# RMSNorm with repeated rows: three-tile runs of stores and loads, wide operations by tile, gamma on the load queue

## The chip, the cores and the metric

The kernel runs on one core of a Trainium2 chip. The metric is the device time of one execution in microseconds, as the median of several runs. A profile of a single execution gives the span from its first to its last recorded event and what every engine and DMA queue did in it.

## The reference

Each row of x (2048 float32) is divided by its root mean square and multiplied by gamma, and each result row stands in the output twice.

```python
x_rep = np.repeat(x, 2, axis=1)                     # x: 8 x 512 x 2048
rms = np.sqrt((x_rep ** 2).mean(axis=-1, keepdims=True) + 1e-6)
return (x_rep / rms * gamma[None, None, :]).astype(np.float32)
```

The input is 33.6 MB and the output, with every row twice, 67.1 MB.

## The kernel before

The 4096 rows are cut into 8 tiles of 512 rows: 128 partitions with K = 4 rows each. A tile has one SBUF buffer `y` of 8 row slots per partition (64 KB). The four x rows are loaded into slots 4 to 7 (L45 to L53); the results go to slots 0, 2, 4 and 6, and their copies to slots 1, 3, 5 and 7, so that x rows are overwritten once they have been used. The whole of the 8 slots is then stored in one piece (L55 to L59). There are three such buffers (L39), so a load of tile j waits for the store of tile j - 3.

The work of one row, by `compute` (L82):

- `square` (L61): ScalarE squares the row into a PSUM scratch tile and sums it at the same time (L64), and takes the root of the mean plus eps (L68).
- `scale` (L71): VectorE takes the reciprocal (L73) and multiplies the row by it and by gamma in one operation (L74).
- `repeat` (L79): ScalarE copies the result into the slot beside it, for the last row of a group VectorE does (L80). ScalarE squares row k + 1 before it copies row k.

The order on each engine is the order of the program (`manual_schedule`, L94); an instruction waits only for what it reads or overwrites. All loads and stores are issued by SyncE (SP) in the order of the program, on one DMA queue, q1: load 0 in two halves, loads 1 and 2, then stores 0 and 1, loads 3 and 4, stores 2 and 3, loads 5 and 6, stores 4 and 5, load 7 in two halves, store 6 and store 7 in two halves (L107 to L116). A store waits on SP for its tile's copies, and what is behind it on SP waits with it. Gamma is one row: ScalarE issues it in four pieces on its own queue, q10 (L97 to L100), and GpSimd broadcasts it to all partitions (L101).

```python
    for i in range(ntiles):
        parts = 2 if i == ntiles - 1 else 1
        for k in range(0, K, K // parts):
            compute(i, k, k + K // parts)
            store(i, k, k + K // parts)

        if i % 2 == 1:
            for j in (i + 2, i + 3):
                if j < ntiles:
                    load(j, nc.sync, parts=2 if j + 1 == ntiles else 1)
```

Of the kernel before, what the change touches and what calls it, by code (L numbers as in the profile page):

```python
# [1 line left out]

# [4 lines left out]


@with_exitstack
def kernel(  # L10
    ctx: ExitStack,
    tc: tile.TileContext,
    x: bass.AP,
    gamma: bass.AP,
    out: bass.AP,
):
    nc = tc.nc
    P = nc.NUM_PARTITIONS
    f32 = mybir.dt.float32
    Act = mybir.ActivationFunctionType  # L20
    Alu = mybir.AluOpType

    B, S, D = x.shape
    Bo, So, Do = out.shape
    R = So // S
    assert R == 2 and D == Do and B == Bo and So == S * R
    eps = 1e-6
    inv_d = 1.0 / float(D)


    K = 4
    N = B * S
    assert N % (P * K) == 0
    ntiles = N // (P * K)
    x_t = x.rearrange("b s d -> (b s) d").rearrange("(n p k) d -> n p k d", p=P, k=K)
    out_t = out.rearrange("b s d -> (b s) d").rearrange("(n p j) d -> n p (j d)", p=P, j=K * R)

    singles = ctx.enter_context(tc.tile_pool(name="singles", bufs=1))
    rows = ctx.enter_context(tc.tile_pool(name="rows", bufs=3))  # L39
    junk = ctx.enter_context(tc.tile_pool(name="junk", bufs=1, space=bass.MemoryType.PSUM))  # L40
    small = ctx.enter_context(tc.tile_pool(name="small", bufs=8))

    ys = []

    def load(i, eng, parts=1):  # L45


        y = rows.tile([P, K * R, D], f32, name="y")
        step = K // parts
        for k in range(0, K, step):  # L50
            at = K * (R - 1) + k
            eng.dma_start(out=y[:, at : at + step, :], in_=x_t[i, :, k : k + step, :])  # L52
        ys.append(y)  # L53

    def store(i, k0, k1):  # L55
        nc.sync.dma_start(  # L56
            out=out_t[i, :, R * k0 * D : R * k1 * D],
            in_=ys[i][:, R * k0 : R * k1, :].rearrange("p j d -> p (j d)"),
        )  # L59

    def square(i, k):  # L61
        sq = junk.tile([P, D], f32, name="sq")
        ss = small.tile([P, 1], f32, name="ss")
        nc.scalar.activation(  # L64
            out=sq[:], in_=ys[i][:, K * (R - 1) + k, :], func=Act.Square, accum_out=ss[:]
        )
        rms = small.tile([P, 1], f32, name="rms")
        nc.scalar.activation(out=rms[:], in_=ss[:], func=Act.Sqrt, scale=inv_d, bias=eps_t[:])  # L68
        return rms

    def scale(i, k, rms):  # L71
        rstd = small.tile([P, 1], f32, name="rstd")
        nc.vector.reciprocal(out=rstd[:], in_=rms[:])  # L73
        nc.vector.scalar_tensor_tensor(  # L74
            out=ys[i][:, R * k, :], in0=ys[i][:, K * (R - 1) + k, :], scalar=rstd[:], in1=gamma_b[:],
            op0=Alu.mult, op1=Alu.mult,
        )

    def repeat(i, k, copy):  # L79
        copy(out=ys[i][:, R * k + 1, :], in_=ys[i][:, R * k, :])  # L80

    def compute(i, k0, k1):  # L82

        rms = square(i, k0)
        for k in range(k0, k1):
            scale(i, k, rms)
            if k + 1 < k1:
                rms = square(i, k + 1)
                repeat(i, k, nc.scalar.copy)
            else:  # L90
                repeat(i, k, nc.vector.tensor_copy)


    ctx.enter_context(tc.manual_schedule())  # L94
    load(0, nc.sync, parts=2)
    gamma_b = singles.tile([P, D], f32, name="gamma_b")
    for c in range(0, D, D // 4):  # L97
        nc.scalar.dma_start(
            out=gamma_b[0:1, c : c + D // 4], in_=gamma[c : c + D // 4].partition_broadcast(1)
        )  # L100
    nc.gpsimd.partition_broadcast(out_ap=gamma_b[:], in_ap=gamma_b[0:1, :])  # L101
    eps_t = singles.tile([P, 1], f32, name="eps_t")
    nc.vector.memset(eps_t, eps)  # L103
    load(1, nc.sync)
    load(2, nc.sync)

    for i in range(ntiles):  # L107
        parts = 2 if i == ntiles - 1 else 1
        for k in range(0, K, K // parts):
            compute(i, k, k + K // parts)  # L110
            store(i, k, k + K // parts)

        if i % 2 == 1:
            for j in (i + 2, i + 3):
                if j < ntiles:
                    load(j, nc.sync, parts=2 if j + 1 == ntiles else 1)  # L116


# [1 line left out]
_INS = ['x', 'gamma']  # L120
_OUTS = [((8, 1024, 2048), 'float32')]


# [23 lines left out]
```

## Time and profile before

| What | Value |
|---|---|
| median of 7 runs | 239.88 us (239.81 to 240.41) |
| the profiled execution | 239.55 us, of which its span is 237.8 us |
| HBM read, written | 33.56 MB, 67.11 MB; 423 GB/s over the span |
| ScalarE (ACT) | 32 squares of 1871 ns, 32 roots of 295, 23 copies of 1888, two table loads of 1283 |
| VectorE (DVE) | 32 scales of 2352 ns, 32 reciprocals of 162, 9 copies of 1226 |
| GpSimd (POOL) | one broadcast of 2292 ns |
| SP waits for copies | 7 times, 121.4 us in all |
| SP waits for an earlier store, before a load | 5 times, 72.8 us in all |

In the profile, each digit of a line of slices is the busy share of 1/40 of the span in tenths. A group of instructions is given as line, engine, operation, output and inputs with their shapes, count, then the busy time in us, the mean of one in ns, and the idle time of the engine before them with what ended most of it. "SPq" is the queue in which SP issues DMAs. A wait of SP is not a loss as such: the DMA engines work on what was issued earlier.

### The profile page before, as it was taken

To read this page: it belongs to the slowest core of one execution; us is meant where nothing else is said; L and a number is where in the kernel's file an instruction comes from. 1 tells how busy PE (TensorE), PEld (TensorE's weight loads), DVE (VectorE), ACT (ScalarE), POOL (GpSimd) and SP (SyncE) were. 2 spreads that over 40 slices of the span, in tenths; PEclk is the share of its full clock that TensorE was granted. 3 is DMA by queue.
4 is the path that set the end of the run, shared out by engine and by line. 5 is a ranking of instruction groups with operands and counts; after the bars stand their busy time and mean duration, and the time that the engine had idled before them with its cause. 6 is when DMAs were issued, how large, how long until landed. Compare 5 with 4: busy or idle time off the path is not lost.

```text
span 237.8 us, 301 instructions
## 1 busy us (share of the span) xinstructions
DVE 90.8 (38%) x74; ACT 115.3 (49%) x121; POOL 2.5 (1%) x5
## 2 busy tenths in 40 slices
DVE  0086977864000084967000007696600009910000
ACT  2699999990000299997000049999500049700000
POOL 0300000000000000000000000000000000000000
DMA  7999998989899999989898999989898999999996
GB/s 265 436 447 441 441 441 353 529 353 507 375 397 436 419 430 437 529 353 529 353 496 353 441 419 442 496 364 518 353 518 364 394 430 499 441 397 419 430 430 265
DMA packets 2746, 100.69 MB, mean 423 GB/s; under 512 B 308, under 2 KB 308, under 8 KB 312
## 3 DMA queue, kind: packets, MB, share of 16 engines
q1 hardware_dynamic: 2736, 100.66, 98.6%
q14 instruction: 2, 0.02, 0.0%
q10 hardware_dynamic: 8, 0.01, 0.0%
HBM read 33.56 MB, written 67.11 MB: 423 GB/s over the span
## 4 chain that ended last, share of the span: by engine, by line
DMA 66%; ACT 15%; DVE 6%; issue 1%; SPq 0%; DVEq 0%
DMA out_dram<-y 40%; DMA y<-in_x_dram 25%; ACT sq L64 7%; ACT y L80 5%; DVE y L74 5%; ACT rms L68 1%; ACT L68 1%; DVE y L80 1%; DVE rstd L73 0%; SPq L52 0%; DVEq L74 0%; SPq L56 0%
## 5 line engine op out<-in xcount | busy, mean ns | idle before, releaser
L64 ACT ACTIVATE sq<-y 128x2048 f32<-128x2048 f32 x32 | 59.9, 1871 | 84.8 <-DMA y<-in_x_dram 84.8
L74 DVE SCALAR_TENSOR_TENSOR y<-y,rstd,gamma_b 128x2048 f32<-128x2048 f32 x32 | 75.3, 2352 | 1.2 <-DVE rstd L73 0.2
L73 DVE RECIPROCAL rstd<-rms 128x1 f32<-128x1 f32 x32 | 5.2, 162 | 115.6 <-ACT rms L68 115.6
L80 ACT COPY y<-y 128x2048 f32<-128x2048 f32 x23 | 43.4, 1888 | 3.7 <-DVE y L74 3.7
L80 DVE COPY y<-y 128x2048 f32<-128x2048 f32 x9 | 11.0, 1226 | 0.3
L68 ACT ACTIVATE rms<-ss,eps_t 128x1 f32<-128x1 f32 x32 | 9.4, 295 | 1.0
L64 ACT ACTIVATION_READ_ACCUMULATOR sq<-y 128x1 f32 x32 | 6.0, 186 | 0.0
L101 POOL PARTITION_BROADCAST gamma_b<-gamma_b x1 | 2.3, 2292 | 8.3 <-DMA gamma_b<-in_gamma_dram 8.3
L64 ACT ACT_TABLE_LOAD x1 | 1.3, 1283 | 2.1 <-issue 2.1
L68 ACT ACT_TABLE_LOAD x1 | 1.3, 1283 | 0.0
L103 DVE MEMSET eps_t<- 128x1 f32 x1 | 0.1, 59 | 0.8 <-PEq L131 0.8
L131 POOL MEMSET const-float32-0.0<- 128x1 f32 x1 | 0.1, 99 | 0.2 <-issue 0.2
L131 POOL MEMSET const-bfloat16-1.0<- 128x1 bf16 x1 | 0.1, 101 | 0.0
L131 POOL MEMSET const-uint8-127<- 128x1 uint8 x1 | 0.1, 101 | 0.0
L131 POOL MEMSET const-float32-1.0<- 128x1 f32 x1 | 0.1, 98 | 0.0
## 6 DMA issues: line engine op xcount, KB each, us to landing
y<-in_x_dram SPq DMA_DIRECT2D x6, 4096.0 KB, 25.0
y<-in_x_dram SPq DMA_DIRECT2D x4, 2048.0 KB, 9.6
out_dram<-y SPq DMA_DIRECT2D x2, 4096.0 KB, 26.6
out_dram<-y SPq DMA_DIRECT2D x7, 31.5
gamma_b<-in_gamma_dram ACTq DMA_DIRECT2D x4, 2.0 KB
```

The lines of the kernel that those rows point to most:

```text
L64: nc.scalar.activation(out=sq[:], in_=ys[i][:, K * (R - 1) + k, :], func=Act.Square, accum_out=ss[:])
L68: nc.scalar.activation(out=rms[:], in_=ss[:], func=Act.Sqrt, scale=inv_d, bias=eps_t[:])
L73: nc.vector.reciprocal(out=rstd[:], in_=rms[:])
L74: nc.vector.scalar_tensor_tensor(out=ys[i][:, R * k, :], in0=ys[i][:, K * (R - 1) + k, :], scalar=rstd[:], in1=gamma_b[:], op0=Alu.mult, o ...
L80: copy(out=ys[i][:, R * k + 1, :], in_=ys[i][:, R * k, :])
L101: nc.gpsimd.partition_broadcast(out_ap=gamma_b[:], in_ap=gamma_b[0:1, :])
L103: nc.vector.memset(eps_t, eps)
L131: nc = _bacc.Bacc("TRN2", target_bir_lowering=False, num_devices=1)
```

## The change

- **Order on SP.** Loads 0 to 2, stores 0 to 2, loads 3 to 5, stores 3 and 4, loads 6 and 7, stores 5 to 7. Only load 0 is still in two halves; store 7, like the others, is one piece.
- **Gamma.** Seven pieces (one of 512 elements, six of 256) on SP's queue: six between the halves of load 0, the last one behind the second half. They land in a small tile of two partitions, and GpSimd broadcasts two halves of 1024 columns.
- **Tables.** ScalarE's table with the square root is loaded ahead of all else, so that the second load of a table falls away. GpSimd sets `eps_t` and a tile of -0.5.
- **Tiles 0 and 3, by rows.** ScalarE sums two rows (Square with accumulation), takes both roots in one operation, and the other two likewise; VectorE takes reciprocals of two columns and scales.
- **Tiles 1, 2, 4, 6 and 7, mixed.** ScalarE squares several rows in one wide operation into slots that are still free (3 rows in tiles 1, 2 and 6; 2 in tile 4; 4 in tile 7) and sums the others as before; VectorE sums the squares in one wide reduce; GpSimd turns the four sums into (mean + eps) ** -0.5 by two small operations on 128x4; VectorE scales the four rows. The sums of the next tile are put into ScalarE's order after the root where `ahead` says so.
- **Tile 5.** All four rows are squared in one operation, reduced by VectorE, and turned by GpSimd; ScalarE scales each row by a Copy with a scale per partition, VectorE multiplies all four by gamma in one operation, and GpSimd makes the copy of all four rows.
- **Copies.** All copies of a tile come after its scales. Tiles 0 and 4: VectorE copies four rows at once. Tiles 1, 2, 3 and 7: ScalarE two, VectorE two. Tile 6: ScalarE two and two.

The diff, cut to its core:

```diff
@@ -42,78 +42,167 @@
     ys = []
-    def load(i, eng, parts=1):
-        y = rows.tile([P, K * R, D], f32, name="y")
-        step = K // parts
-        for k in range(0, K, step):
-            at = K * (R - 1) + k
-            eng.dma_start(out=y[:, at : at + step, :], in_=x_t[i, :, k : k + step, :])
-        ys.append(y)
-    def store(i, k0, k1):
+    def new_tile():
+        ys.append(rows.tile([P, K * R, D], f32, name="y"))
+    def load(i, k0, k1):
         nc.sync.dma_start(
-            out=out_t[i, :, R * k0 * D : R * k1 * D],
-            in_=ys[i][:, R * k0 : R * k1, :].rearrange("p j d -> p (j d)"),
-        )
-    def square(i, k):
+            out=ys[i][:, K * (R - 1) + k0 : K * (R - 1) + k1, :], in_=x_t[i, :, k0:k1, :]
+        )
+    def store(i):
+        nc.sync.dma_start(out=out_t[i], in_=ys[i].rearrange("p j d -> p (j d)"))
+    H = K // 2
+    x_at = K * (R - 1)
+    def total(i, k, ss):
         sq = junk.tile([P, D], f32, name="sq")
-        ss = small.tile([P, 1], f32, name="ss")
         nc.scalar.activation(
-            out=sq[:], in_=ys[i][:, K * (R - 1) + k, :], func=Act.Square, accum_out=ss[:]
-        )
-        rms = small.tile([P, 1], f32, name="rms")
-        nc.scalar.activation(out=rms[:], in_=ss[:], func=Act.Sqrt, scale=inv_d, bias=eps_t[:])
-        return rms
-    def scale(i, k, rms):
-        rstd = small.tile([P, 1], f32, name="rstd")
-        nc.vector.reciprocal(out=rstd[:], in_=rms[:])
-        nc.vector.scalar_tensor_tensor(
-            out=ys[i][:, R * k, :], in0=ys[i][:, K * (R - 1) + k, :], scalar=rstd[:], in1=gamma_b[:],
-            op0=Alu.mult, op1=Alu.mult,
-        )
-    def repeat(i, k, copy):
-        copy(out=ys[i][:, R * k + 1, :], in_=ys[i][:, R * k, :])
-    def compute(i, k0, k1):
-        rms = square(i, k0)
+            out=sq[:], in_=ys[i][:, x_at + k, :], func=Act.Square, accum_out=ss[:, k : k + 1]
+        )
+    def square(i, k0, k1):
+        nc.scalar.activation(
+            out=ys[i][:, k0:k1, :], in_=ys[i][:, x_at + k0 : x_at + k1, :], func=Act.Square
+        )
+    def reduce(i, k0, k1, ss):
+        nc.vector.tensor_reduce(
+            out=ss[:, k0:k1], in_=ys[i][:, k0:k1, :], op=Alu.add, axis=mybir.AxisListType.X
+        )
+    def root(k0, k1, ss):
+        at = ss[:, k0:k1]
+        nc.gpsimd.tensor_scalar(
+            out=at, in0=at, scalar1=inv_d, scalar2=eps, op0=Alu.mult, op1=Alu.add
+        )
+        nc.gpsimd.tensor_tensor(out=at, in0=at, in1=power_t[:, k0:k1], op=Alu.pow)
+    def scale(i, k0, k1, rstd):
         for k in range(k0, k1):
-            scale(i, k, rms)
-            if k + 1 < k1:
-                rms = square(i, k + 1)
-                repeat(i, k, nc.scalar.copy)
-            else:
-                repeat(i, k, nc.vector.tensor_copy)
+            nc.vector.scalar_tensor_tensor(
+                out=ys[i][:, R * k, :], in0=ys[i][:, x_at + k, :], scalar=rstd[:, k : k + 1],
+                in1=gamma_b[:], op0=Alu.mult, op1=Alu.mult,
+            )
+    def repeat(i, k0, k1, copy=nc.scalar.copy):
+        y_r = ys[i].rearrange("p (k r) d -> p k r d", r=R)
+        copy(out=y_r[:, k0:k1, 1, :], in_=y_r[:, k0:k1, 0, :])
+    def columns():
+        return small.tile([P, K], f32, name="ss")
     ctx.enter_context(tc.manual_schedule())
-    load(0, nc.sync, parts=2)
+    assert ntiles == 8
     gamma_b = singles.tile([P, D], f32, name="gamma_b")
-    for c in range(0, D, D // 4):
-        nc.scalar.dma_start(
-            out=gamma_b[0:1, c : c + D // 4], in_=gamma[c : c + D // 4].partition_broadcast(1)
-        )
-    nc.gpsimd.partition_broadcast(out_ap=gamma_b[:], in_ap=gamma_b[0:1, :])
+    cuts = [0, *range(D // 4, D + 1, D // 8)]
+    for _ in range(3):
+        new_tile()
+    gamma_row = singles.tile([64, D // 2], f32, name="gamma_row")
+    def gamma_half(c):
+        at = 32 * (c // (D // 2))
+        return gamma_row[at : at + 1, :]
+    def gamma_piece(c0, c1):
+        at = c0 % (D // 2)
+        nc.sync.dma_start(
+            out=gamma_half(c0)[:, at : at + c1 - c0], in_=gamma[c0:c1].partition_broadcast(1)
+        )
+    power_t = singles.tile([P, K], f32, name="power_t")
+    nc.gpsimd.memset(power_t, -0.5)
     eps_t = singles.tile([P, 1], f32, name="eps_t")
-    nc.vector.memset(eps_t, eps)
-    load(1, nc.sync)
-    load(2, nc.sync)
-    for i in range(ntiles):
-        parts = 2 if i == ntiles - 1 else 1
-        for k in range(0, K, K // parts):
-            compute(i, k, k + K // parts)
-            store(i, k, k + K // parts)
-        if i % 2 == 1:
-            for j in (i + 2, i + 3):
-                if j < ntiles:
-                    load(j, nc.sync, parts=2 if j + 1 == ntiles else 1)
+    nc.gpsimd.memset(eps_t, eps)
+    nc.scalar.preload_act_table(Act.Sqrt)
+    load(0, 0, H)
+    for c0, c1 in zip(cuts[:-2], cuts[1:-1]):
+        gamma_piece(c0, c1)
+    load(0, H, K)
+    gamma_piece(cuts[-2], cuts[-1])
+    for c0 in (0, D // 2):
+        nc.gpsimd.partition_broadcast(out_ap=gamma_b[:, c0 : c0 + D // 2], in_ap=gamma_half(c0))
+    load(1, 0, K)
+    load(2, 0, K)
+    def root_quick(k0, k1, ss):
+        at = ss[:, k0:k1]
+        nc.scalar.activation(out=at, in_=at, func=Act.Sqrt, scale=inv_d, bias=eps_t[:])
+        nc.vector.reciprocal(out=at, in_=at)
+    def by_rows(i, copies):
+        ss = [columns() for _ in range(R)]
+        for h, k0 in enumerate(range(0, K, H)):
+            for k in range(k0, k0 + H):
+                total(i, k, ss[h])
+            root_quick(k0, k0 + H, ss[h])
+            scale(i, k0, k0 + H, ss[h])
+        for k0, k1, copy in copies:
+            repeat(i, k0, k1, copy)
+        store(i)
+    def sums(i, by_row):
+        ss = columns()
+        square(i, by_row, K)
+        for k in range(by_row):
+            total(i, k, ss)
+        return i, by_row, ss
+    def mixed(given, copies, ahead=None):
+        i, by_row, ss = given
+        reduce(i, by_row, K, ss)
+        root(0, K, ss)
+        if ahead is not None:
+            ahead = sums(*ahead)
+        scale(i, 0, K, ss)
+        for k0, k1, copy in copies:
+            repeat(i, k0, k1, copy)
+        store(i)
+        return ahead
+    whole = ((0, K, nc.vector.tensor_copy),)
+    shared = ((0, H, nc.scalar.copy), (H, K, nc.vector.tensor_copy))
+    by_scalar = ((0, H, nc.scalar.copy), (H, K, nc.scalar.copy))
+    by_rows(0, whole)
+    two = mixed(sums(1, 1), shared, ahead=(2, 1))
+    mixed(two, shared)
+    for j in (3, 4, 5):
+        new_tile()
+        load(j, 0, K)
+    by_rows(3, shared)
+    _, _, ss = mixed(sums(4, H), whole, ahead=(5, 0))
+    for j in (6, 7):
+        new_tile()
+        load(j, 0, K)
+    reduce(5, 0, K, ss)
+    root(0, K, ss)
+    for k in range(K):
+        nc.scalar.activation(
+            out=ys[5][:, R * k, :], in_=ys[5][:, x_at + k, :], func=Act.Copy, scale=ss[:, k : k + 1]
+        )
+    y_r = ys[5].rearrange("p (k r) d -> p k r d", r=R)
+    nc.vector.tensor_tensor(
+        out=y_r[:, :, 0, :], in0=y_r[:, :, 0, :],
+        in1=gamma_b[:].rearrange("p (k d) -> p k d", k=1).to_broadcast([P, K, D]), op=Alu.mult,
+    )
+    repeat(5, 0, K, nc.gpsimd.tensor_copy)
+    store(5)
+    last = mixed(sums(6, 1), by_scalar, ahead=(7, 0))
+    mixed(last, shared)
 # ---- launch: one core; inputs and outputs as the reference has them ----
```

## The prediction

> **What bounds the kernel now.** I read the page first: engine shares, the slices and the queue.
>
> ```profile
> span 237.8 us, 301 instructions
> ...
> DVE 90.8 (38%) x74; ACT 115.3 (49%) x121; POOL 2.5 (1%) x5
> ...
> DMA  7999998989899999989898999989898999999996
> ...
> q1 hardware_dynamic: 2736, 100.66, 98.6%
> ```
>
> No compute engine is busy half the span; the one DMA queue, q1, holds the 16 DMA engines for 98.6% of it. Next, the stages, in the view by windows (length, busy time of DVE, ACT and POOL with counts, PE clock, DMA share, GB/s):
>
> ```profile
> 1.70:3.00 1.30, 0.00 (x0) 0.91 (x1) 0.00 (x0) 1.00 0.96 227
> ...
> 72.00:88.00 16.00, 3.90 (x4) 5.87 (x7) 0.00 (x0) 1.00 1.00 430
> 92.00:128.00 36.00, 16.26 (x13) 18.78 (x20) 0.00 (x0) 1.00 1.01 437
> 130.00:146.00 16.00, 3.61 (x4) 5.58 (x7) 0.00 (x0) 1.00 1.00 430
> 150.00:186.00 36.00, 16.56 (x13) 19.07 (x20) 0.00 (x0) 1.00 1.01 437
> ...
> 235.00:237.80 2.80, 0.00 (x0) 0.00 (x0) 0.00 (x0) 1.00 0.11 47
> ```
>
> Loads alone (72 to 88, 130 to 146) run at 430 GB/s and stores alone at 437, with compute beside them or not. So neither the direction nor the engines set the rate. Only the start (227 GB/s) and the end are below it. Last, the queue's own issues in order of time:
>
> ```profile
> 26.54 15.13 SPq L56 DMA_DIRECT2D out_dram<-y  x2
> 52.65 19.92 SPq L52 DMA_DIRECT2D y<-in_x_dram  x2
> 72.74 26.27 SPq L56 DMA_DIRECT2D out_dram<-y  x2
> 110.93 19.74 SPq L52 DMA_DIRECT2D y<-in_x_dram  x2
> 130.78 26.52 SPq L56 DMA_DIRECT2D out_dram<-y  x2
> 169.15 1.35 SPq L52 DMA_DIRECT2D y<-in_x_dram  x2
> ```
>
> The second load of the first pair was issued at 72.24 (store 1 complete), and the load at 130.34 when store 3 was complete: 58.1 us for two loads and two stores. The trace's records of single packets give the same. Each engine moves a whole-tile load as 8 packets of 1.213 us (9.70), a store as 8 of 2.418 (19.34), a half-tile load as 8 of 0.611 (4.89); 2 x (9.70 + 19.34) = 58.1. There is no hole: every transfer is queued before its turn. Data runs from 1.75 to 236.5 us. Eight loads and eight stores at these prices are 232.3, so in the whole kernel only some 5.5 us are not streaming: 1.75 before the first byte, about 0.6 of slow first packets, 0.93 at the first store (the last loads before it are slow), about 0.06 at each later turn from loads to stores, the spread of the engines, and 1.26 after the last byte. ScalarE's waits for loads cost nothing.
>
> [...]
>
> **The change, part by part.** Prices come from these groups:
>
> ```profile
> L64 ACT ACTIVATE sq<-y 128x2048 f32<-128x2048 f32 x32 | 59.9, 1871 | 84.8 <-DMA y<-in_x_dram 84.8
> L74 DVE SCALAR_TENSOR_TENSOR y<-y,rstd,gamma_b 128x2048 f32<-128x2048 f32 x32 | 75.3, 2352 | 1.2 <-DVE rstd L73 0.2
> ...
> L80 ACT COPY y<-y 128x2048 f32<-128x2048 f32 x23 | 43.4, 1888 | 3.7 <-DVE y L74 3.7
> L80 DVE COPY y<-y 128x2048 f32<-128x2048 f32 x9 | 11.0, 1226 | 0.3
> ```
>
> *Bytes.* Unchanged. Load 7 whole saves 16 x 0.611 - 8 x 1.213 = 0.07 us an engine, store 7 whole 16 x 1.213 - 8 x 2.418 = 0.06, two DMAs fewer 0.02 of completion packets. One turn from loads to stores fewer (3 for 4, the costly first one stays): 0.06. Sum -0.21.
>
> *Gamma.* Four row pieces on ACT's queue become seven on SP's, behind load 0a. A 2 KB piece took 84 + 9 ns on one engine, so 0.37 becomes 0.42 (1 KB at half) to 0.65: +0.05 to +0.28 on one of 16 engines; I take +0.05. Seven more issues on SP at some 0.3 to 0.4 us delay load 0b to about 3.3 us, with 0a streaming until 7: hidden. The last piece lands behind load 0b near 12.6 instead of before 8.8, so the second half-broadcast (about 1.2) ends near 14 and tile 0's scaling starts at 14 instead of 12.1. ACT no longer shares the first issues: the first load's packets may then start closer together, between 0 and -0.4; I take -0.1.
>
> *Order and compute.* The order S0 S1 S2 L3 L4 L5 S3 S4 L6 L7 S5 S6 S7 costs nothing only while each store is ready before the queue runs dry. Continuing from store 0 complete at 52.65, completions fall at S1 72.0, S2 91.3, L3 101.0, L4 110.7, L5 120.4, S3 139.8, S4 159.1, L6 168.8, L7 178.5, S5 197.8, S6 217.2. A store must be issued about 1.0 us ahead (first issue 0.72, first byte 1.75), and completion is noticed 0.35 (loads) to 0.65 (stores) after the last byte. So lateness counts from S0 31.9, S1 51.0, S2 70.3, S3 119.0, S4 138.1, S5 177.1, S6 196.1, S7 215.5; the earliest engine is idle some 1.2 us sooner, which doesn't move the end. On SP every load also waits for the store that frees its buffer: load 5 for store 2 (complete 91.3, its turn is 110.7), load 7 for store 4 (159.1, turn 168.8), with stores 3 and 5 queued behind these waits but not due before 119 and 177: nothing.
> [...] Four scales are 9.45. The root on POOL, two operations on 128x4 with three hand-overs, shows in no row: at least 0.3 (memset 0.10 each), at most 2.3 (the broadcast); I take 0.6. DVE's scales and all its later work queue behind it.
> Tile 0: scales from 14.0, the second pair after ACT's sums at 17, to 23.6; DVE copies 4 rows to 28.1; limit 31.9. Tile 1: loaded 22.6, squares to 27.9, reduce from 28.2 to 34.7, root 35.4, scales 44.9, DVE copy 47.2; limit 51.0. Tile 2: reduce to 53.8, root, scales 64, copy 66.3; limit 70.3. Tile 3 (loaded 101.0): two sums 105.0, root 105.5, two scales 110.3, two more 115.3, DVE copy 117.6, while ACT copies its two rows 110.4 to 114.0; limit 119.0. Tile 4: ACT squares 114.0 to 117.6, sums to 121.6; reduce to 122.1, root 122.8, scales 132.2, copy 136.7; limit 138.1. Tile 5: reduce to 145.4, root 146, four ACT copies with scale 153.7, DVE multiply by gamma 162.4, [...]; limit 177.1. Tile 6 (168.8): squares 174.2, reduce 180.8, root 181.4, scales 190.9, ACT copy 194.5; limit 196.1. Tile 7: reduce 199.6, scales 209.7, copies 212.0; limit 215.5. All are in time, tiles 3, 4 and 6 by only 1.4 to 1.6. The removed root and table-load work (9.4 of 0.295 us roots, one 1283) was never on the path: worth nothing.
>
> **Sum.** -0.21 + 0.05 - 0.1 = -0.26: span 237.5. The profiled execution took 239.55, 1.75 more than its span, and the median is 0.33 above it: 239.88 - 0.26 = 239.6.
>
> **Rivals.** (A) *The start collapses*: engines start together and the first packets no longer run slow; up to 0.4 of stagger plus part of the 0.6, with the 0.21: 239.2. For: the start is the one thin stage. Against: the first packets take 1.1 to 1.5 us for 0.61 even where gamma isn't in the way. (B) *The queue runs dry at store 4*, the other side. ACT's tile-4 squares stand behind its tile-3 copy. If that copy waits for all four scales, it runs 115.3 to 118.9, squares end 122.5, sums 126.5, and with root, scales and copy tile 4 is ready at 141.1, 3.0 after the limit, store 6 about 1.8 late as well but absorbed only if its limit has moved by the 3.0: 242.6. A slow root does the same from R = 2.0 us; at 2.3 it costs 0.3. For: in the present trace no ACT copy stands on strided rows. Against: the first half of tile 0 is squared at 8.1 while its other half is still landing, so waits go by rows. (C) *POOL's copy for tile 5 is late*: it decides from 14.7 us, 1.8 ns an element; [...] For: POOL's rate isn't in the trace. Against: [...] the broadcast's 1.1 ns an element.
>
> **Chances.** My forecast, all stores in time, 0.56, with its own range 239.3 to 240.0; A 0.17; B 0.18, some of it small overruns of 0.5 to 2; C 0.09. About 0.2% (0.48 us) is what a measurement of this kernel can tell from no change: faster 0.21, same 0.49, slower 0.30. Low 239.1 takes in A; high 242.0 leaves out the full 3 us of B and C.
>
> **What would show it.** The slices of DMA all at 9 or 8 after the first; no window with a share below 0.95 at 119, 138, 177 and 196 us; stores 3, 4 and 6 issued near 117.7, 136.8 and 194.6; POOL's 128x4 operations under 1 us in sum; its 8192 copy under 14 us. A hole before store 3, 4, 5 or 6 makes the forecast wrong, as does a first byte earlier than 1.5 us.

## The result and the profile after

The changed kernel takes **242.88 us** (median of 12 runs, 242.09 to 244.16), the kernel before 239.94 in the same comparison: a ratio of 1.012, 95% interval 1.0106 to 1.0133. It is slower by 2.9 us. The forecast was 239.6 with a range up to 242.0; the time lies above it. The execution that was profiled took 242.11 us, one of the quickest of the twelve and 2.6 us more than the profiled one of before, so the trace shows most of the loss and not all of it.

The page of the changed kernel, its heading, engine shares, slices and queue:

```profile
span 240.3 us, 230 instructions
...
DVE 133.2 (55%) x45; ACT 90.7 (38%) x47; POOL 17.2 (7%) x21
...
DMA  7999999999999999999999999899999999999994
...
q1 hardware_dynamic: 2462, 100.67, 98.3%
```

The reader is to see what is not there: no slice with a hole. The DMA engines look as busy as before, 98.3% for 98.6, and yet the same bytes take 2.5 us of span more. So most of the loss is not in a queue that stands empty; the packets themselves take longer, as the account below shows.

The queue's own issues, in order of time (start, time to the end of the last one of the group, what):

```profile
28.80 40.08 SPq L56 DMA_DIRECT2D out_dram<-y  x3
68.97 23.94 SPq L51 DMA_DIRECT2D y<-in_x_dram  x3
118.73 19.98 SPq L56 DMA_DIRECT2D out_dram<-y  x2
140.97 19.76 SPq L51 DMA_DIRECT2D y<-in_x_dram  x2
171.95 42.79 SPq L56 DMA_DIRECT2D out_dram<-y  x3
```

Store 3 was issued at 118.7 and store 4 at 138.4 (118.73 + 19.98 less the 0.34 of an issue); the forecast had 117.7 and 136.8. The new operations, as groups (count, then busy us and mean ns of one, then the engine's idle time before them and its releaser; "+2 forms" means that the mean mixes three shapes):

```profile
L74 DVE TENSOR_REDUCE ss<-y 128x3 f32<-128x6144 f32 (+2 forms) x6 | 41.4, 6904 | 11.1 <-ACT y L69 11.0
L69 ACT ACTIVATE y<-y 128x6144 f32<-128x6144 f32 (+2 forms) x6 | 33.6, 5604 | 27.6 <-DMA y<-in_x_dram 27.6
...
L80 POOL TENSOR_SCALAR ss<-ss 128x4 f32<-128x4 f32 x6 | 1.2, 194 | 156.5 <-DVE ss L74 156.5
L94 POOL COPY y<-y 128x8192 f32<-128x8192 f32 x1 | 7.0, 7009 | 16.6 <-DVE y L197 16.6
L83 POOL TENSOR_TENSOR ss<-ss,power_t 128x4 f32<-128x4 f32 x6 | 6.1, 1017 | 0.5
```

And, from the timeline, the moments at which loads 1, 3, 6 and 7 release ScalarE; the line at 124.58 is tile 4's first scale, which waited 1.48 us for the root on GpSimd:

```profile
23.85 5.33 ACT L69 ACTIVATE y<-y 128x6144 f32<-128x6144 f32 x1 [6.21 <-DMA y<-in_x_dram]
...
102.28 1.88 ACT L63 ACTIVATE sq<-y 128x2048 f32<-128x2048 f32 x1 [37.09 <-DMA y<-in_x_dram]
...
124.58 9.26 DVE L87 SCALAR_TENSOR_TENSOR y<-y,ss,gamma_b 128x2048 f32<-128x2048 f32 x4 [1.48 <-POOL ss L83]
...
170.10 5.32 ACT L69 ACTIVATE y<-y 128x6144 f32<-128x6144 f32 x1 [13.98 <-DMA y<-in_x_dram]
...
181.27 7.03 ACT L69 ACTIVATE y<-y 128x8192 f32<-128x8192 f32 x1 [3.96 <-DMA y<-in_x_dram]
```

The forecast had 22.6, 101.0, 168.8 and 178.5 for the loads. In the trace's records of packets the last of the 16 DMA engines ends its part of these loads at 23.50, 101.85, 169.69 and 180.86, 0.35 to 0.43 us ahead of these moments; the mean of the 16 ends at 22.33, 100.52, 169.30 and 180.06. So that last engine is 1.25 us late by load 1, keeps this lag to load 6, and loses another 1.5 between loads 6 and 7; the end then comes 2.8 us after the forecast's span of 237.5. It lost nothing at stores 3 and 4, though both were issued late: its ends went from 121.21 (load 5) to 140.53 and 159.85, 19.32 us for each store, as long as 8 of the quickest packets (19.34). What was lost there fell on engines that were ahead of it: for the earliest the first of these steps took 19.91.

**The account.** The trace's records of single packets give each packet's start and length. A turn is the point at which the queue goes from loads to stores or back. Against the quickest lengths (0.611, 1.213 and 2.418 us for 16, 32 and 64 KB), packets after the first 4 us ran long by 1.16 us per DMA engine in the kernel before and by 3.02 in the changed one. Between its packets a DMA engine stood idle for 0.10 and 0.41. At these lengths the fewer, larger packets save 0.14 (232.46 us per engine for 232.59). The mean of the 16 engines' last ends moved from 235.98 to 238.01, the last of them from 236.51 to 238.81. Where packets ran long (us per engine):

| Turn | before | changed |
|---|---|---|
| load 1, its last packets | 0.00 | 0.26 |
| load 2 to store 0 | 0.93 | 0.74 |
| later turns from loads to stores | 0.07, 0.07, 0.05 | load 5 to store 3: 0.00 (idle 0.17), load 7 to store 5: 1.06 |
| turns from stores to loads | 0.00 to 0.01 | store 2 to load 3: 0.07; store 4 to load 6: 0.63 (idle 0.15 ahead of store 4) |

### The profile page after: what moved, and what is told of

Read it like the earlier page. It is cut to its first block, busy times and chain, and to the rows that moved or that the text cites. A ratio compares the mean times of both kernels' runs of the same rounds, so it can differ in the third digit from the quotient of the medians.

```text
span 240.3 us, 230 instructions
## 1 busy us (share of the span) xinstructions
DVE 133.2 (55%) x45; ACT 90.7 (38%) x47; POOL 17.2 (7%) x21
## 3 DMA queue, kind: packets, MB, share of 16 engines
q1 hardware_dynamic: 2462, 100.67, 98.3%
## 5 line engine op out<-in xcount | busy, mean ns | idle before, releaser
L87 DVE SCALAR_TENSOR_TENSOR y<-y,ss,gamma_b 128x2048 f32<-128x2048 f32 x28 | 64.8, 2349 | 9.9 <-POOL ss L83 7.4
L74 DVE TENSOR_REDUCE ss<-y 128x3 f32<-128x6144 f32 (+2 forms) x6 | 41.4, 6904 | 11.1 <-ACT y L69 11.0
L69 ACT ACTIVATE y<-y 128x6144 f32<-128x6144 f32 (+2 forms) x6 | 33.6, 5604 | 27.6 <-DMA y<-in_x_dram 27.6
L63 ACT ACTIVATE sq<-y 128x2048 f32<-128x2048 f32 x13 | 24.4, 1874 | 44.1 <-DMA y<-in_x_dram 43.9
L94 ACT COPY y<-y 128x4096 f32<-128x4096 f32 x6 | 21.6, 3602 | 28.9 <-DVE y L87 28.9
L94 DVE COPY y<-y 128x4096 f32<-128x4096 f32 (+1 forms) x6 | 18.0, 3004 | 0.2
L193 ACT ACTIVATE y<-y,ss 128x2048 f32<-128x2048 f32 x4 | 7.8, 1994 | 18.8 <-POOL ss L83 18.8
L197 DVE TENSOR_TENSOR y<-y,gamma_b 128x8192 f32<-128x8192 f32 x1 | 8.7, 8691 | 9.3 <-ACT y L193 9.3
L94 POOL COPY y<-y 128x8192 f32<-128x8192 f32 x1 | 7.0, 7009 | 16.6 <-DVE y L197 16.6
L83 POOL TENSOR_TENSOR ss<-ss,power_t 128x4 f32<-128x4 f32 x6 | 6.1, 1017 | 0.5
```

Of the source, the lines that this page charges most:

```text
L63: nc.scalar.activation(out=sq[:], in_=ys[i][:, x_at + k, :], func=Act.Square, accum_out=ss[:, k : k + 1])
L69: nc.scalar.activation(out=ys[i][:, k0:k1, :], in_=ys[i][:, x_at + k0 : x_at + k1, :], func=Act.Square)
L74: nc.vector.tensor_reduce(out=ss[:, k0:k1], in_=ys[i][:, k0:k1, :], op=Alu.add, axis=mybir.AxisListType.X)
L83: nc.gpsimd.tensor_tensor(out=at, in0=at, in1=power_t[:, k0:k1], op=Alu.pow)
L87: nc.vector.scalar_tensor_tensor(out=ys[i][:, R * k, :], in0=ys[i][:, x_at + k, :], scalar=rstd[:, k : k + 1], in1=gamma_b[:], op0=Alu.mul ...
L94: copy(out=y_r[:, k0:k1, 1, :], in_=y_r[:, k0:k1, 0, :])
```

## The experiments

The theory that I began with: stores 3 and 4 come late, the queue runs dry, and the engines, which start again together, then lose more at each turn. Rivals: a transfer issued shortly before its turn slows those ahead of it; gamma on the load queue disturbs the first loads; later, that slow turns belong to addresses, to the order of transfers, or to where the buffers lie in SBUF. All ratios are to the kernel before.

**Load 3 in halves.**

```diff
     for j in (3, 4, 5):
         new_tile()
-        load(j, 0, K)
+        step = H if j == 3 else K
+        for k0 in range(0, K, step):
+            load(j, k0, k0 + step)
```

> The changed kernel with load 3 in two halves, so that tile 3 can start some 4.8 us sooner and stores 3 and 4 are queued before their turn. Theory 1 (the queue runs dry at stores 3 and 4, and engines that restart together lose more at the switches at 159 and 179 us): the 0.3 us of idle engines and the 0.6 and 1.1 us of slow packets go, about 240.9. Theory 2 (a transfer issued less than some 8 us before its turn slows the packets ahead of it): store 5 keeps its lead of 7.7 us and its 1.1 us, stores 3 and 4 gain short leads, so 242.2 to 243. Theory 3 (gamma on the load queue disturbs the first loads): no change but the 0.3 us, 242.5.

Measured: 241.89, ratio 1.0085 (1.0072 to 1.0099). Its queue:

```profile
114.43 21.66 SPq L56 DMA_DIRECT2D out_dram<-y  x2
141.44 19.69 SPq L51 DMA_DIRECT2D y<-in_x_dram  x2
169.34 45.78 SPq L56 DMA_DIRECT2D out_dram<-y  x3
```

Stores 3 and 4 are now issued at 114.4 and 135.8 and neither finds an idle engine; the turns from store 4 to load 6 (0.03) and from load 7 to store 5 (0.22) are cheap. By the medians that is 1.0 us of the 2.9. Yet its engines are about 2.4 us apart from store 0 on, where the kernel before has 0.6, and store 6, issued at 196.8, found the earliest of them done: 0.57 us idle. Packets run long by 1.56 us, only 0.40 more than before. So of the 2.0 us that are left, long packets and the late store 6 explain about 0.9; the rest is the last engine, which ends 1.8 us after the mean of the 16, where it was 0.5 before. Lateness is a part, not the whole.

**The order alone** (row work and gamma as before), **gamma alone**, and **both with row work**.

```diff
-    for i in range(ntiles):
-        parts = 2 if i == ntiles - 1 else 1
...
+    then = {2: (3, 4, 5), 4: (6, 7)}
+    for i in range(ntiles):
+        compute(i, 0, K)
+        store(i, 0, K)
+        for j in then.get(i, ()):
+            load(j, nc.sync)
```

> The kernel before with the new order of stores and loads and an undivided last tile alone; rows are still worked one by one, so tiles 4 to 7 are ready 10 us and more ahead. Theory 1: store 3 is issued near 118, about its turn, a small idle stretch at most, 239.9 to 240.5. Theory 2: all later leads are long, 239.8. If runs of three loads and three stores cost by themselves, 241 or more.

Measured: 240.59, 1.0047 (1.003 to 1.0065). Store 3 at 118.1 finds no idle engine, but packets ran long by 0.22 before load 6 and by 0.89 before store 5, without any dry stretch. So a dry stretch is not needed for a slow turn; the second half of my theory fails here. Nine of the 13 executions took 240.2 to 240.9 us and four 241.4 to 242.4.

> The kernel before with gamma's seven pieces on SP's queue, the two half broadcasts and the early table load alone. Theories 1 and 2: within 0.2 of the kernel before, 239.9. Theory 3: slow packets in loads 1 and 2, +0.3 to +0.6, 240.3.

Measured: 240.41, 1.0015 (0.9999 to 1.003): at most 0.7 us. In its trace the first turn is quick (0.06) and the turn from load 4 to store 2 slow (0.86) in its place. Loads 1 and 2 are not disturbed (443, 440 and 440 GB/s in the slices from 12 to 30 us; before 447, 441 and 441); the rival on gamma fails.

> New order and new gamma with the row by row work of before on all tiles. If the parts add up: 239.9 + 0.65 + 0.5 = 241.1, and the wide work owns the remaining 1.8 us. If gamma and the order together make store 3 late (gamma delays tile 0 to 2 by 2.4 us, but not tile 3): no more than 241.3. If it is 242.5 or more, the wide work is cleared.

Measured: 239.86, 1.001 (0.9994 to 1.0026): no difference from the kernel before that this can tell, at most 0.6 us. It is a sum of things that cancel: the two slow turns of the new order (0.39 and 0.77) are there, and the first one (0.01) is gone. Nor is it one time: 14 of the 22 executions took 239.4 to 240.0 us and eight took 240.5 to 241.9. The trace is of one of the 14 (239.62), and none shows where the eight lost their time. Still, the longest of them is shorter than the shortest of the changed kernel (242.09). The expectation's 241.1 was wrong, and its conclusion holds more strongly: the change's 3 us come with the edit that brings the new work on the tiles.

**Transfers alone**, in both orders; what is left of the work is VectorE's zeroing and the broadcast of gamma.

```diff
     def compute(i, k0, k1):
-        rms = square(i, k0)
-        for k in range(k0, k1):
...
+        if k0 == 0:
+            nc.vector.memset(ys[i][:, 0:K, :], 0.0)
```

> The transfers of the kernel before alone: squares, roots, scales and copies are left out, VectorE only zeroes the four lower row slots of each tile (the output is x and zeros). If slow turns come from the work beside the transfers: no slow turn, the 0.93 us of the first store goes, 239.0. If they belong to the transfers: 239.9.

> The same with the new order (three stores, three loads, two, two, three; last tile whole), the arithmetic left out likewise. If slow turns come from the work beside: 238.9, equal to the old order within 0.2. If the order itself makes the turn from load 7 to store 5 slow: 0.6 to 0.9 above the old order.

Measured: old order 239.95, ratio 1.000 (0.9988 to 1.0011); new order 239.61, 0.9979 (0.9972 to 0.9987). The kernel before is therefore as fast as its transfers alone, slow first turn (1.07) included. The new order is faster by 0.21% as long as there is no work beside it: in its trace the turns at loads 6 and 7 cost 0.01 and 0.08, though the first turn cost 1.31. The same order with row work had 0.22 and 0.89 at loads 6 and 7, though store 5 was issued at 160.1 in both. The rival "the order itself makes these turns slow" fails. Two causes are left, the work beside the transfers and the later issue of stores 3 and 4 that it brings. Their issues in this run were at 101 and 111:

```profile
101.46 10.07 SPq L56 DMA_DIRECT2D out_dram<-y  x2
```

With row work in the same order they were at 118 and 133:

```profile
118.12 15.13 SPq L56 DMA_DIRECT2D out_dram<-y  x2
```

**The new work under the old order.** First as a plain exchange of the order:

> The changed kernel's work on the tiles with the order of loads and stores and the gamma of before (tile 0's load in halves, the last tile whole). Every store is ready several us ahead. If the wide operations cost only by making stores late, this is 239.9; if they disturb the transfers by themselves (the engines spread apart from load 1 on in the changed kernel), 240.5 or more.

Measured: 271.73. That was the experiment's own fault: in ScalarE's order tile 7's squares stand ahead of tile 6's copies, and in the old order load 7 comes only behind stores 4 and 5. Its timeline:

```profile
183.63 9.27 DVE L87 SCALAR_TENSOR_TENSOR y<-y,ss,gamma_b 128x2048 f32<-128x2048 f32 x4 [2.02 <-POOL ss L83]
213.75 7.03 ACT L69 ACTIVATE y<-y 128x8192 f32<-128x8192 f32 x1 [40.23 <-DMA y<-in_x_dram]
220.69 7.09 ACT L94 COPY y<-y 128x4096 f32<-128x4096 f32 x2
...
227.81 0.33 SPq L56 DMA_DIRECT2D out_dram<-y  x1
```

Tile 6's rows were scaled at 192.9; its copies waited behind squares that waited for load 7, and store 6 went out at 227.8. The new work as it stands is tied to the new order. With tile 7's squares behind tile 6's copies, and tiles 5 and 7 by rows:

> The order and the gamma of before with the changed kernel's work on tiles 0 to 4 and 6, and rows two by two on tiles 5 and 7 (tile 5's and 7's own way takes longer than the old order leaves them; tile 7's sums no longer stand ahead of tile 6's copies, which had made that order take 271.7). All stores are in time. If the wide operations cost only by late stores: 239.9 to 240.2. If they disturb the transfers themselves: 240.5 or more.

Measured: 242.24, 1.0098 (1.0085 to 1.0112). Store 7 was late (issued at 216.6; 0.84 us idle), so the premise that all are in time was not met. Packets ran long by 1.64 (before: 1.16), and the engines were 2.0 us apart at store 0 and more than 3 at the end of store 6. The new work costs under the old order too, but this run can't say how much of its 2.2 us is the late store and how much the spread of the engines.

**Gamma of before in the changed kernel; tile 0's new work alone in the kernel before.**

> The changed kernel with gamma as before (four pieces on ACT's queue, one broadcast). If the parts add up (order alone +0.7, gamma alone +0.5, the rest by late stores), about 242.4; if gamma is what spreads the engines in load 1 and makes loads 3 to 5 land 1.2 us late, stores 3 and 4 are in time and it falls to 240.6 to 241.

Measured: 243.26, 1.0153 (1.0136 to 1.0169). Gamma neither spreads the engines nor delays the stores: load 1 runs long by 0.20 here too.

> The kernel before with tile 0 alone done as in the changed kernel (two rows at a time, then one wide VectorE copy of four rows). If tile 0's new work drives the engines apart: first starts of store 0 spread over 2 us in place of 0.6, and 240.3 to 240.8. If not: 239.9 and a spread of 0.6.

Measured: 239.96, 0.9996 (0.9986 to 1.0007), engines 0.6 apart. It isn't tile 0.

This bears on the wide operations too. In the changed kernel load 1's long packets start between 19.7 and 21.7 us, and the first wide operation starts at 23.85; with gamma of before it is 17.3 to 20.5 and 22.9. What runs until then is tile 0's work by rows, which costs nothing here. So wide operations that run beside the transfers can't have begun the spread. In the traces, nearly all that parts the changed kernel from the one with new order, new gamma and row work stands early: the last DMA engine finishes load 2 at 34.2 us in the one and 32.3 in the other (before: 32.9), and its last byte follows at 238.8 and 236.7 (before: 236.5). With load 3 in halves it is 34.6 and 238.7.

**Time of issue.** In the kernel before, load 6 in halves and, ahead of store 4:

```diff
             compute(i, k, k + K // parts)
+            if i == 4:
+                nc.gpsimd.tensor_copy(out=ys[4][:, 1, 0:1], in_=ys[6][:, K, 0:1])
             store(i, k, k + K // parts)
```

> The kernel before with load 6 in two halves and store 4 held back until the first half has landed (GpSimd writes one element of that half into column 0 of one output row slot of tile 4, which is therefore wrong). Store 4 is then issued about 4 us before its turn in place of 17, with no idle stretch. Theory 1: no change, 239.9. Theory 2: the last packets of load 6 run 0.7 to 1.0 us slow, 240.7.

Measured: 240.03, 1.0003 (0.9994 to 1.0013); store 4 was issued 3 us before its turn and the turn cost 0.06. A lead of 3 us costs nothing at this turn.

The leads in the changed kernel were shorter, though. Over all traces of the new order, the two slow turns go with the lead of store 3, from its issue to the first byte that an engine moves for it (us; long packets per engine):

| Kernels with the new order | lead of store 3 | store 4 to load 6 | load 7 to store 5 |
|---|---|---|---|
| changed (two traces), and its variants with old gamma, rows exchanged, buffers 32 bytes back | 0.8 to 0.9 | 0.61 to 0.66 | 0.83 to 1.08 |
| row work: order alone, with rows exchanged, with new gamma | 1.2 to 1.5 | 0.18 to 0.39 | 0.60 to 0.89 |
| changed, load 3 in halves | 4.9 | 0.03 | 0.22 |
| transfers alone | 18.2 | 0.01 | 0.08 |

Only the run with load 3 in halves moves this lead by intent and leaves the work as it is, so this is a pattern with one experiment behind it. It is not a mechanism: store 5, whose turn is the slowest, was itself issued 7.5 us ahead or more. What passes from store 3 to the later turns was not tried.

**The same programs again, and other rows.**

> The kernel before once more, for a second trace of it. In its first trace one of four turns from loads to stores was slow (0.93 us at the first store) and three were quick (0.04 to 0.07). If slow turns belong to the program and its addresses, the same one is slow again, by 0.9. If they fall by chance, another or none is.

> The changed kernel once more, for a second trace. In its first trace the turns at 159 us (0.63) and 179 us (1.06) were slow and the queue ran dry at 118 and 138 us (0.17 and 0.15). If slow turns belong to the program, both come again; if they fall by chance, the span differs by about 1 us a turn. The dry stretches come again in any case.

Measured, one execution each: 239.57 with the slow turn at store 0 again (0.99; the others 0.03 to 0.07), and 242.75 with 0.26 at load 1, 0.73, 0.62 and 1.08 at the same turns as in the first trace. In these two pairs of traces the slow turns come again with the program. The two groups of times of the new order with row work show that one program need not always run alike.

```diff
+    at_tile = [1, 0, 2, 3, 4, 5, 6, 7]
...
-in_=x_t[i, :, k : k + step, :]
+in_=x_t[at_tile[i], :, k : k + step, :]
```

> The kernel before with tiles 0 and 1 of the tensors exchanged (the first tile worked on is rows 512 to 1023, the second rows 0 to 511); every instruction, wait and time of issue stays. Two traces of the kernel before have the same single slow turn, 0.93 and 0.99 us at the first store. Theory A (a turn is slow when the HBM addresses of the tail of the load and of the head of the store lie badly to each other; the pairs load tile a, store tile b were slow for 8b - 4a of -8 and 12 MB and quick for 0, 4, 8 and 20): the pair (2, 1) has 0, the turn is quick, 239.0. Theory B (it belongs to the first store or to the moment): it stays slow, 239.9.

> The new order alone, with the tiles of the tensors taken in the order 1 0 2 3 5 4 7 6, so that all three turns from loads to stores have the differences 0, 8 and 8 that were quick. Theory A: the 1.06 and 0.89 us of the run with the order alone go, 238.8. Theory B: 240.6 as there.

> The changed kernel with the tiles of the tensors taken in the order 1 0 2 3 5 4 7 6. Theory A: the slow turns (0.73, 0.62 and 1.08 in its second trace) go or shrink, and with the first of them stores 3 and 4 are no later than before against their turn: 240.5 to 241.3. Theory B: 242.9 as before.

Measured: 239.92, 241.52 and 243.47 (ratios 0.9998, 1.0052 and 1.0136; intervals 0.999 to 1.0006, 1.0029 to 1.0074, 1.0115 to 1.0157). The slow turns stayed where they were (0.93; 0.87 and 0.60; 0.93, 0.62 and 0.83). It is not which rows a tile holds. My table of address differences was a pattern in too few points.

**The buffers 32 bytes further, or back.** The kernels that spread were also the ones whose row buffers lie 32 bytes further on.

```diff
+    pad_t = singles.tile([P, 1], f32, name="pad_t")
+    nc.vector.memset(pad_t, 0.0)
```

> The kernel before with one more 4-byte tile in the pool ahead of the row buffers, which moves these from byte 24736 to 24768 of each partition; all work and all transfers stay. If the placement slows the transfers: slow packets before 8 us, engines 2 us apart at store 0, 240.6 to 241.8. If it is the wide work: 239.9 and a spread of 0.6 us.

> The changed kernel with the tile of -0.5 and the tile of eps put into one, which moves the row buffers from byte 28864 to 28832, where the run with new order and new gamma had them; all work and all transfers stay. If the placement slows the transfers: the spread and the slow packets of load 1 go, load 3 lands near 101 in place of 102.3, stores 3 and 4 are in time, and the turn at 178 may stay slow by 0.8: 239.6 to 240.6. If it is the wide work: 242.9 as before.

Measured: 239.89, 1.0001 (0.9991 to 1.001), and 243.42, 1.0139 (1.0115 to 1.0163), with the spread unchanged in both (0.6 and 2.4 us at store 0). A neat correlation, and no cause.

## Why the prediction was wrong

- **What bounds the kernel: right.** With the arithmetic left out, the transfers in the old order take as long as the kernel before (ratio 1.000).
- **Bytes and turns, -0.21: right only without the work.** The new order with the arithmetic left out is 0.21% faster, 0.3 to 0.4 us by the medians. The step that failed is the term "one turn from loads to stores fewer: 0.06", together with what it assumed silently, that packets keep the lengths of the trace before. There were three turns from loads to stores in place of four, but they cost 0.74, 0.00 and 1.06 us in place of 0.93 and some 0.06 each; the turn from store 4 to load 6, put at nothing, cost 0.63, and load 1 another 0.26. Long packets rose by 1.86 us per engine. I took the equal rates of long stretches (430 and 437 GB/s) to mean that work beside the transfers doesn't slow them, at the turns either. No run here tests that at the turns: the new order with row work (240.59) and without (239.61) differ in the lead of store 3 as well, 1.3 us and 18.2.
- **Gamma: not contradicted.** New gamma beside the new order shows no cost, but no run can tell the forecast's 0.05 from nothing. The second half of gamma came later than forecast, tile 0's scaling at 14.85 for 14.0, which stayed hidden. The first byte came no earlier to speak of (1.73 for 1.75) and the first packets were no quicker (the first 16 took 1.20 us on the mean, before 1.14), so the -0.1 for the start was not there.
- **Order and compute: durations near those of the schedule, margins too thin.** The schedule's durations for work wider than a row, and for GpSimd's copy, were assumed: the trace before has none of them. A square of three rows took 5.32 us where the schedule has 5.3 (22.6 to 27.9), a reduce of three 6.55 for 6.5 (28.2 to 34.7), VectorE's copy of four rows 4.43 for 4.5 (23.6 to 28.1), and four scales 9.26 for 9.45. GpSimd's copy took 7.01, where up to 14.7 would have done. The root was mis-sized: 0.19 + 1.02 us, 1.5 from reduce to first scale, where I took 0.6. With load 3 landing 1.3 late, stores 3 and 4 came 1.0 and 1.6 later than forecast: store 3 within 0.3 of its limit, store 4 0.3 past it. I let lateness count only from the last of the DMA engines; idle time of the earlier ones was 0.17 and 0.15 us on the mean. The last one indeed lost nothing there, but the short lead went with the slow turns that followed. Load 3 in halves won back 1.0 us by the medians.
- **Rivals.** B, the queue running dry at store 4, had the right side and a late store 4, but not its mechanism: ScalarE's copy for tile 3 ran at 111.5, beside the last scales, and did not wait for them. That its 242.6 is close to the time measured is luck. C fell (7.0 us, where it decides from 14.7), and so did A.
- **The spread.** I treated the engines' distance, about 1 us at the end before, as slack. In every kernel with the new work on tiles 0 to 4 they were about 2 to 2.7 us apart from store 0, so the last one ends later and the first finds a late store sooner.

**What is shown, and what stays open.** The 3 us come with the edit that puts the new work on the tiles: the rest of the change, run together, has the median of before (1.001, at most 0.6 us more). Of them, 1.0 goes when stores 3 and 4 are no longer late. The rest is mostly engines that drift apart in the first 34 us, and its cause is not settled. It is not the rows' addresses, gamma, tile 0's new work by itself, or a shift of the buffers by 32 bytes. It begins ahead of the wide operations, and some of it ahead of any work on a tile: in the changed kernel packets that start between 5.4 and 6.3 us ran long by 0.07 us per engine. Which part of the edit does it was not tried. Nor did any run settle why one turn costs 0.9 and the next 0.06, even with transfers alone; moving gamma moved the slow one from store 0 to store 2. The time of issue isn't cleared either: a lead of 3 us did no harm at one turn, and the leads of about 1 us, which go with the slow turns, were not varied by themselves. The best version with full work that ran is no faster than the kernel before.

## What to carry to other kernels

A kernel that is as fast as its transfers alone (here 239.94 us and 239.95) has nothing to gain from cheaper work, and can lose from work that is ready just in time (242.88, and 241.89 with store 3 issued 4.3 us and store 4 2.6 us sooner): leave each store a margin larger than the error of your schedule. Here the error was 1.0 to 1.6 us and the margin 1.4 to 1.6. Before work is rebuilt for a better order of transfers, run that order with the arithmetic left out, and then with the old work; here the first gained 0.2% and the second had lost it again.

When the busy share stays where it was (here 98.6% and 98.3%) and the time grows (by 2.9 us), compare the lengths of single packets at the turns, and the end of the last DMA engine and not only their mean: a busy queue can be a slow one (long packets of 3.02 us per engine for 1.16).

## What the hardware showed unexpectedly

- A turn between loads and stores cost anything from 0.00 to 1.3 us per DMA engine. In the dear ones the last one or two packets of most engines ran 0.2 to 1.3 us long. The same turns were dear in both traces of a program, and another one in a program that differs in how gamma is loaded and in an early table load.
- A distance between the DMA engines, once there, lasted: the 2.0 us of the run with the new work in the old order at store 0 were still there 100 us later, at load 5. In the changed kernel it was 2.4 us at store 0 and 2.1 at load 5; behind stores 3 and 4, for which the earlier engines had to wait, it was 0.6.
- GpSimd copied 128x8192 float32 in 7.01 us (0.86 ns an element) and took 1.02 us for a power on 128x4.
- The effects of the parts did not simply add. By the medians the order alone cost 0.7 us and gamma alone 0.5 (its interval reaches 0); both together lie between -0.1 and +0.6.
